# Thin fp32 products of a hybrid decoder block: one 128-row matmul instead of two 64-row matmuls

## Chip, cores and metric

One core of a Trainium2 chip runs the whole program; the seven others are idle. The metric is device time in microseconds of one execution. The engines are named as in the profile: PE is TensorE (PEld its weight loads), DVE is VectorE, ACT is ScalarE, POOL is GpSimd, SP is SyncE.

## The reference, cut

2048 tokens of width 1024 pass through one layer, all in fp32:

```
z  = rmsnorm(x) @ W_in                    # 1024 -> GLA heads | RWKV-7 heads
o  = concat(gla(z), rwkv7(z)) @ W_out;    h  = x + o
h += relu(rmsnorm(h) @ W1)^2 @ W2         # 1024 -> 4096 -> 1024
h += sigmoid(rmsnorm(h) @ W_g) * (p @ W_ple)
out = rmsnorm(h)
```

`gla` is gated linear attention with 4 heads (keys of 64, values of 128). `rwkv7` has 8 heads of 64 and the recurrence `S_t = S_{t-1} (diag(w_t) - kk_t^T (a_t kk_t)) + v_t^T k_t`. Both are computed in chunks with a carried state.

## The kernel before

The tokens form 4 blocks of 512; activations are held transposed, features on partitions and 512 tokens along the free dimension. Each large product is a `panel` (L287): 8 pieces of the contraction, each three matmuls in float32r (`mm3`, L278 to L280: high by high, high by low, low by high), 128x128 weights against 512 columns. So PE's stream is mostly L278, L279, L280 over and over.

A program of units sets the order. Per block these are the projection (`z_units`, tiles named z0 to z3), the output projection (o0 to o3), the feed-forward part (f0 to f3) and the gated embedding (p0 to p3). The chunked mixers are cut into small steps (`rwkv_units`, tiles r00 to r33; `gla_units`, g00 to g33; the digits are block and job, 16 jobs of 128 tokens each). A `tick` after each half panel lets the mixers' next steps in, so short groups of small matmuls stand between panels. The mixers of block 0 run beside the projections of blocks 1 to 3 (up to about 850 us); those of blocks 1, 2 and 3 beside the o, f and p parts of blocks 0, 1 and 2; the last block's o, f and p run alone.

The small fp32 products with 128 output rows went through a helper, `thin` (L282 to L284), which splits the 128 stationary columns in two: output rows 0 to 63 and 64 to 127, one matmul each. Four places call it:

- `Norm.sums` (L316): 4 products per call with one moving column (`ones1`). It gives the sums of squares of an RMSNorm; 16 calls, 4 per block.
- the post step of `rw_k` (L485): 4 products per call with 2 moving columns (`bo2`); 16 calls, all in the projections.
- `load` of `gla_units` (L627): 2 products with 2 moving columns, 16 calls; four transposes (L638) follow it.
- `chain` of `rwkv_units` (L955): 8 products, one per head, with 64 moving columns: the state and values in `P2` (tiles rpe, rpo) under weights in `W2` (rwe, rwo). 2 chains per job, 32 calls. ACT then copies the result (L957).

In the trace every fp32 matmul is two records on PE and two weight loads on PEld, one for each of its passes; float32r has one. Other small products that matter here use the array in other ways: L652 (128 stationary columns, 128 moving, fp32, full array), L735 (64 stationary columns), L638 and L763 (transposes by the identity).

Of the kernel before, what the change touches and what calls it, by code (L numbers as in the profile page):

```python
# [17 lines left out]
P = 128  # L18
# [43 lines left out]
def tile_hybrid_block(ctx: ExitStack, tc: tile.TileContext, a: dict, out: bass.AP):  # L62
    nc = tc.nc
    V, A, G, T = nc.vector, nc.scalar, nc.gpsimd, nc.tensor
# [7 lines left out]
    def st(shape, tag, bufs, dtype=F32):  # L72
        counter[0] += 1
        return sb.tile(shape, dtype, tag=tag, bufs=bufs, name=f"{stage[0]}.{tag}_{counter[0]}")
# [6 lines left out]
    def g2(n=TB):  # L81
        return st([P, 520], "g2", 10)[:, :n]
# [7 lines left out]
    def gx(n=512):  # L90
        return pt("gx", 4, n)

    def ct(shape, name, dtype=F32):
        return const.tile(shape, dtype, tag=name, name=name)
# [18 lines left out]
    ones1 = ct([P, 1], "ones1")  # L113
# [5 lines left out]
    bo2 = ct([P, 2], "bo2")  # L119
# [11 lines left out]
    for half in range(2):  # L131
        for q in range(4):
            m = mask[64 * half : 64 * half + 64, 64 * q : 64 * q + 64]
# [83 lines left out]
    def rsqrt(v, n, tag):  # L217
        half = st([P, n], tag + "i", 1, I32)
        V.tensor_scalar(half, v.bitcast(I32), 1, None, ALU.logical_shift_right)
        yi = st([P, n], tag + "y", 2, I32)  # L220
        V.tensor_scalar(yi, half, -1, RSQRT_MAGIC, ALU.mult, ALU.add)
        y = yi.bitcast(F32)
        t = st([P, n], tag + "t", 1)
        for _ in range(3):
            V.tensor_tensor(out=t, in0=y, in1=y, op=ALU.mult)
            V.scalar_tensor_tensor(t, t, -0.5, v, ALU.mult, ALU.mult)
            V.scalar_tensor_tensor(y, t, 1.5, y, ALU.add, ALU.mult)
        return y
# [50 lines left out]
        T.matmul(acc, wh, xs[1], start=False, stop=False)  # L279
        T.matmul(acc, wl, xs[0], start=False, stop=stop)  # L280

    def thin(acc, w, x):  # L282
        for m in (0, 64):
            T.matmul(acc[m : m + 64], w[:, m : m + 64], x, start=True, stop=True)  # L284

    def panel(w, xs, m=P):
        acc = pt("mm", 4)  # L287
        for k in range(KT):
            mm3(acc[:m], w, k, xs[k], k == 0, k == KT - 1, m)
            if k == KT // 2 - 1:  # L290
                tick()
        return acc

    class Norm:
# [18 lines left out]
        def sums(self):  # L313
            c = gx(4)
            for t in range(4):
                thin(c[:, t : t + 1], self.acc[:, t * P : t * P + P], ones1)  # L316
            v = st([P, 4], "nv", 2)
            V.tensor_scalar(v, c, 1.0 / D, EPS, ALU.mult, ALU.add)
            self.y = rsqrt(v, 4, "nr")
# [15 lines left out]
    def z_units(b):  # L335
# [37 lines left out]
        def project(m=P):  # L373
            return panel(take_w(), z["xs"], m)
# [99 lines left out]
        def rw_k(p):  # L474
            def f():
                k = shift(normed(project()), P, RW_K - RW_R + p)
                cols = slice(p * P, p * P + P)

                kq = g2()
                A.activation(kq, k, AF.Square, scale=vc("k_k", p))  # L480

                def post():
                    sp = gx(8)
                    for t in range(4):
                        thin(sp[:, 2 * t : 2 * t + 2], kq[:, t * P : t * P + P], bo2)  # L485
                    v = st([P, 8], "rnv", 1)
                    V.tensor_scalar(v, sp, 1e-24, None, ALU.max)
                    iv = rsqrt(v, 8, "rr")
                    ib = g2()
                    V.tensor_copy(ib.rearrange("p (t e) -> p t e", e=64), iv.unsqueeze(2).to_broadcast([P, 8, 64]))  # L490
                    pa = gx()
                    T.matmul(pa, a2s[:, cols], z["as"], start=True, stop=True)
                    an = g2()
                    A.activation(an, pa, AF.Tanh, bias=a0h[:, p : p + 1], scale=0.5)
                    kf = g2()
                    A.activation(kf, an, AF.Identity, bias=ka1[:, p : p + 1], scale=kah[:, p : p + 1])
                    A.activation(an, an, AF.Copy, bias=-0.5, scale=-0.5)
                    V.tensor_tensor(out=kf, in0=kf, in1=k, op=ALU.mult)
                    yield
                    ivb = gx()  # L500
                    for t in range(4):
                        T.transpose(ivb[:, t * P : t * P + P], ib[:, t * P : t * P + P], ident)
                    kkn = g2()
                    V.scalar_tensor_tensor(kkn, k, vc("k_k", p), ivb, ALU.mult, ALU.mult)
                    V.tensor_tensor(out=an, in0=an, in1=kkn, op=ALU.mult)
                    z["kkn"], z["an"], z["kf"] = kkn, an, kf

                return post

            return f  # L510
# [99 lines left out]
    def gla_units(b, j):  # L610
# [4 lines left out]
        def load():  # L615
            q, k, bb = (st([P, 2, P], n, 1) for n in ("gq", "gk", "gb"))
            ld(q, d_gq[b][:, :, js])
            ld(k, d_gk[b][:, :, js])
            ld(bb, d_gb[b][:, :, js])
            v = st([P, 4, P], "gv", 1)  # L620
            ld(v, d_gv[b][:, :, js])
            s_.update(q=q, k=k, b=bb)
            dp = gx(4)
            qk = st([P, 2, P], "gqk", 3)
            V.tensor_tensor(out=qk, in0=q, in1=k, op=ALU.mult)
            for i in range(2):
                thin(dp[:, 2 * i : 2 * i + 2], qk[:, i], bo2)  # L627
            ds = st([P, 4], "gds", 1)
            V.tensor_copy(ds, dp)
            S_ = st([P, 4, P], "gS", 1)  # L630
            V.tensor_tensor(
                out=S_, in0=ident.unsqueeze(1).to_broadcast([P, 4, P]),
                in1=ds.unsqueeze(2).to_broadcast([P, 4, P]), op=ALU.mult,
            )
            s_["S"] = S_
            bank = gx()
            for h in range(4):
                T.transpose(bank[:, h * P : h * P + P], v[:, h], ident)  # L638
            vt = st([P, 4, P], "gvt", 1)
            A.copy(vt.rearrange("p h e -> p (h e)"), bank)  # L640
            s_["vt"] = vt
# [142 lines left out]
    def rwkv_units(b, j):  # L784
# [158 lines left out]
        def chain(c):  # L943
            def f():
                yr, xr = halves[c], halves[1 - c]
                P2 = (s_["pe"], s_["po"])
                W2 = (s_["we"], s_["wo"])
                heads = [(h, *divmod(h, 2)) for h in range(8)]
                if c == 0:
                    A.copy(P2[0][lo, 0], rst[lo])  # L950
                    A.copy(P2[1][hi, 0], rst[hi])
                    s_["y"] = st([P, 512], "ry", 1)
                xy = pt("gx", 4)
                for h, p, e in heads:
                    thin(xy[:, h * 64 : h * 64 + 64], W2[e][:, p, c], P2[e][:, c, p])  # L955
                xs = st([P, 512], "rxs", 1)
                A.copy(xs, xy)  # L957
                yield
                ub = pt("gx", 4, 256)
                for h, p, e in heads:  # L960
                    T.matmul(ub[halves[e], p * 64 : p * 64 + 64], TT[xr, h], xs[xr, h * 64 : h * 64 + 64], start=True, stop=True)
                uv = ub.rearrange("z (p e) -> z p e", p=4)
                A.copy(P2[0][lo, c], uv[lo])
                V.tensor_copy(P2[1][hi, c], uv[hi])
                yield
                db = gx(256)
                for h, p, e in heads:
                    T.matmul(db[halves[e], p * 64 : p * 64 + 64], s_["bkt"][:, p, c, e], P2[e][:, c, p], start=True, stop=True)
                wt = st([P, 4, 64], "rwt", 1)
                V.tensor_tensor(out=wt, in0=rst, in1=db.rearrange("z (p e) -> z p e", p=4), op=ALU.add)  # L970
                pcb = pcs[b][:, :, 2 * j + c : 2 * j + c + 1].to_broadcast([P, 4, 64])
                if c == 0:
                    V.tensor_tensor(out=P2[0][lo, 1], in0=wt[lo], in1=pcb[lo], op=ALU.mult)
                    V.tensor_tensor(out=P2[1][hi, 1], in0=wt[hi], in1=pcb[hi], op=ALU.mult)
                V.tensor_tensor(out=rst, in0=wt, in1=pcb, op=ALU.mult)
                y2 = gx(256)
                for h, p, e in heads:
                    er = halves[e]
                    T.matmul(y2[er, p * 64 : p * 64 + 64], s_["gb"][er, p, c, 64 * c : 64 * c + 64], P2[e][er, c, p], start=True, stop=True)
                for e in range(2):  # L980
                    V.tensor_tensor(
                        out=hv(s_["y"][yr])[:, e], in0=hv(xs[yr])[:, e],
                        in1=y2[halves[e]].rearrange("z (p n) -> z p n", n=64), op=ALU.add)

            return f
# [338 lines left out]
```

## Time and profile before

| | |
|---|---|
| median of 3 runs | 2967.32 us (2962.82 to 2969.42) |
| the profiled execution | 2965.06 us, span 2963.4 us |
| PE busy | 2861.0 us (97%) |
| DVE, ACT busy | 2213.3 us (75%), 1189.7 us (40%) |
| granted TensorE clock, mean | 0.984 |
| fp32 records on the helper's line L284 | 1664 on PE, 1664 on PEld |

A matmul's record begins when it is dispatched and ends as the profile models it; records overlap. How long a group of matmuls holds PE is therefore read from the starts: from the start of the last panel matmul ahead of it to the start of the second panel matmul behind it, less the two panel steps that would have been there without it.

### The profile page before, as it was taken

To read this page: it belongs to the slowest core of one execution; us is meant where nothing else is said; L and a number is where in the kernel's file an instruction comes from. 1 tells how busy PE (TensorE), PEld (TensorE's weight loads), DVE (VectorE), ACT (ScalarE), POOL (GpSimd) and SP (SyncE) were. 2 spreads that over 40 slices of the span, in tenths; PEclk is the share of its full clock that TensorE was granted. 3 is DMA by queue.
4 is the path that set the end of the run, shared out by engine and by line. 5 is a ranking of instruction groups with operands and counts; after the bars stand their busy time and mean duration, and the time that the engine had idled before them with its cause. 6 is when DMAs were issued, how large, how long until landed. Compare 5 with 4: busy or idle time off the path is not lost.

```text
span 2963.4 us, 46550 instructions
## 1 busy us (share of the span) xinstructions
PE 2861.0 (97%) x16856; PEld 2264.1 (76%) x16856; DVE 2213.3 (75%) x5417; ACT 1189.7 (40%) x2230; POOL 114.1 (4%) x321
## 2 busy tenths in 40 slices
PE   7889999999999999999999999999999999999997
PEld 5667777777777877787777878777878787888886
DVE  6878786968797767788877868797867787544455
ACT  5435445444343333344433334443333344322233
POOL 4330000000000000000000000000000000000000
PEclk9999999999999999999999999999999999999999
DMA  7896877776754333334533333454333334322222
GB/s 277 291 310 207 251 231 224 244 231 211 231 182 121 106 117 114 115 111 154 147 113 110 111 116 107 127 176 118 109 116 114 103 108 164 100 94 99 93 94 78
DMA packets 332552, 453.63 MB, mean 153 GB/s; under 512 B 134096, under 2 KB 216064, under 8 KB 332320
## 3 DMA queue, kind: packets, MB, share of 16 engines
q1 hardware_dynamic: 324832, 423.38, 46.1%
q0 software_dynamic: 7488, 27.27, 2.3%
q8 instruction: 133, 2.18, 0.3%
q14 instruction: 99, 0.81, 0.1%
HBM read 357.21 MB, written 93.32 MB: 152 GB/s over the span
## 4 chain that ended last, share of the span: by engine, by line
PE 65%; DVE 7%; DMA 1%; issue 1%; SPq 1%; ACT 1%; DVEq 0%; ACTq 0%
PE f1.mm L278 4%; PE f3.mm L279 4%; PE f3.mm L278 4%; PE f3.mm L280 4%; PE f1.mm L280 4%; PE f1.mm L279 4%; PE f0.mm L278 3%; PE f2.mm L278 3%; PE f2.mm L280 3%; PE f2.mm L279 3%; PE f0.mm L280 3%; PE f0.mm L279 3%; PE p0.mm L278 1%; PE p1.mm L278 1%; PE p3.mm L278 1%
## 5 line engine op out<-in xcount | busy, mean ns | idle before, releaser
L251 ACT CAST f3.w<-f3.wr 128x512 fp32r<-128x512 f32 x128 | 79.6, 622 | 204.6 <-PE f3.mm L280 197.8
L251 ACT CAST f0.w<-f0.wr 128x512 fp32r<-128x512 f32 x128 | 79.1, 618 | 165.9 <-PE f0.mm L280 129.7
L251 ACT CAST f2.w<-f2.wr 128x512 fp32r<-128x512 f32 x128 | 79.0, 618 | 153.3 <-PE f2.mm L280 128.4
L251 ACT CAST f1.w<-f1.wr 128x512 fp32r<-128x512 f32 x128 | 79.0, 618 | 152.8 <-PE f1.mm L280 126.5
L254 DVE TENSOR_TENSOR f3.w<-f3.wr,f3.w 128x512 fp32r<-128x512 f32 x128 | 88.6, 692 | 63.1 <-ACT f3.w L251 59.8
L254 DVE TENSOR_TENSOR f0.w<-f0.wr,f0.w 128x512 fp32r<-128x512 f32 x128 | 88.0, 687 | 27.6 <-ACT f0.w L251 27.1
L254 DVE TENSOR_TENSOR f1.w<-f1.wr,f1.w 128x512 fp32r<-128x512 f32 x128 | 87.9, 686 | 24.5 <-ACT f1.w L251 23.9
L254 DVE TENSOR_TENSOR f2.w<-f2.wr,f2.w 128x512 fp32r<-128x512 f32 x128 | 87.9, 687 | 24.1 <-ACT f2.w L251 23.4
L278 PE MATMUL f1.mm<-f1.x,f1.w 128*128 128x512 f32 x256 | 103.7, 405 | 0.0
L278 PE MATMUL f2.mm<-f2.x,f2.w 128*128 128x512 f32 x256 | 103.6, 405 | 0.0
L278 PE MATMUL f0.mm<-f0.x,f0.w 128*128 128x512 f32 x256 | 103.5, 404 | 0.0
L280 PE MATMUL f1.mm<-f1.x,f1.w 128*128 128x512 f32 x256 | 101.4, 396 | 0.0
L280 PE MATMUL f0.mm<-f0.x,f0.w 128*128 128x512 f32 x256 | 101.3, 396 | 0.0
L279 PE MATMUL f1.mm<-f1.x,f1.w 128*128 128x512 f32 x256 | 101.1, 395 | 0.0
L280 PE MATMUL f2.mm<-f2.x,f2.w 128*128 128x512 f32 x256 | 101.1, 395 | 0.0
L279 PE MATMUL f0.mm<-f0.x,f0.w 128*128 128x512 f32 x256 | 100.9, 394 | 0.0
L280 PE MATMUL f3.mm<-f3.x,f3.w 128*128 128x512 f32 x256 | 100.8, 394 | 0.0
L278 PE MATMUL f3.mm<-f3.x,f3.w 128*128 128x512 f32 x256 | 100.7, 394 | 0.0
L279 PE MATMUL f2.mm<-f2.x,f2.w 128*128 128x512 f32 x256 | 100.7, 393 | 0.0
L278 PE MATMUL f0.mm<-o0.x,f0.w 128*128 128x512 f32 x248 | 100.7, 406 | 0.0
L279 PE MATMUL f3.mm<-f3.x,f3.w 128*128 128x512 f32 x256 | 100.6, 393 | 0.0
L278 PE MATMUL f2.mm<-o2.x,f2.w 128*128 128x512 f32 x248 | 100.2, 404 | 0.0
(2799 smaller groups left out, 8844.5 us busy)
## 6 DMA issues: line engine op xcount, KB each, us to landing
f0.wr<-w SPq DMA_DIRECT2D x63, 512.0 KB, 3.4
f1.wr<-w SPq DMA_DIRECT2D x63, 512.0 KB, 3.4
f2.wr<-w SPq DMA_DIRECT2D x63, 512.0 KB, 3.4
f3.wr<-w SPq DMA_DIRECT2D x63, 512.0 KB, 3.3
wc<-z0.w POOLq DMA_DIRECT2D x52, 512.0 KB, 5.5
z1.w<-wc SPq DMA_DIRECT2D x52, 512.0 KB, 5.3
z2.w<-wc SPq DMA_DIRECT2D x52, 512.0 KB, 4.8
z3.w<-wc SPq DMA_DIRECT2D x50, 512.0 KB, 4.4
```

Source lines behind the costliest of these rows:

```text
L251: A.copy(t[:, :512], r)
L254: eng.tensor_tensor(out=t[:, 512:], in0=r, in1=t[:, :512], op=ALU.subtract)
L278: T.matmul(acc, wh, xs[0], start=start, stop=False)
L279: T.matmul(acc, wh, xs[1], start=False, stop=False)
L280: T.matmul(acc, wl, xs[0], start=False, stop=stop)
```

## The change

The helper goes, and each of its four callers issues one matmul with all 128 stationary columns and all 128 output rows. Operands, moving columns, output places and the number of products stay; 832 half matmuls become 416 whole ones.

```diff
-    def thin(acc, w, x):
-        for m in (0, 64):
-            T.matmul(acc[m : m + 64], w[:, m : m + 64], x, start=True, stop=True)
...
-                thin(c[:, t : t + 1], self.acc[:, t * P : t * P + P], ones1)
+                T.matmul(c[:, t : t + 1], self.acc[:, t * P : t * P + P], ones1, start=True, stop=True)
...
-                        thin(sp[:, 2 * t : 2 * t + 2], kq[:, t * P : t * P + P], bo2)
+                        T.matmul(sp[:, 2 * t : 2 * t + 2], kq[:, t * P : t * P + P], bo2, start=True, stop=True)
...
-                thin(dp[:, 2 * i : 2 * i + 2], qk[:, i], bo2)
+                T.matmul(dp[:, 2 * i : 2 * i + 2], qk[:, i], bo2, start=True, stop=True)
...
-                    thin(xy[:, h * 64 : h * 64 + 64], W2[e][:, p, c], P2[e][:, c, p])
+                    T.matmul(xy[:, h * 64 : h * 64 + 64], W2[e][:, p, c], P2[e][:, c, p], start=True, stop=True)
```

Four lines fewer shift every later line number by 4: L955 is L951 after the change.

A scheduler decides where the small groups stand. It leaves the groups in their places beside the panels but for shifts by a panel matmul or two, nearly all in the projections. On PE, in the feed-forward part of block 0, a chain's eight products stand between two panel matmuls. Before (sizes are output rows x moving columns; f0.mm is a panel's accumulator, r10.gx the chain's result):

```order
L280 MATMUL f0.mm_9824<-o0.x_9422,f0.w_9735 128x512
L284 MATMUL r10.gx_9879<-r10.rpe_8884,r10.rwe_8867 64x64 x2
L284 MATMUL r10.gx_9879<-r10.rpo_8885,r10.rwo_8868 64x64 x2
L284 MATMUL r10.gx_9879<-r10.rpe_8884,r10.rwe_8867 64x64 x2
L284 MATMUL r10.gx_9879<-r10.rpo_8885,r10.rwo_8868 64x64 x2
...
L278 MATMUL f0.mm_9906<-o0.x_8928,f0.w_9816 128x512
```

And the same place with the change:

```order
L280 MATMUL f0.mm_9666<-o0.x_9268,f0.w_9577 128x512
L951 MATMUL r10.gx_9721<-r10.rpe_8732,r10.rwe_8715 128x64
L951 MATMUL r10.gx_9721<-r10.rpo_8733,r10.rwo_8716 128x64
L951 MATMUL r10.gx_9721<-r10.rpe_8732,r10.rwe_8715 128x64
L951 MATMUL r10.gx_9721<-r10.rpo_8733,r10.rwo_8716 128x64
...
L278 MATMUL f0.mm_9740<-o0.x_8774,f0.w_9658 128x512
```

The group keeps its place; each pair of 64-row matmuls has become one of 128 rows.

In four jobs the chain's group stands right behind another group with 64 stationary columns (L735, L731 after the change), here on PE in the gated embedding of block 0. Before:

```order
L731 MATMUL g13.gx_13809<-gst,g13.gqk_13663 128x128
L735 MATMUL g13.gx_13818<-g13.gvt_12936,g13.gk_13659 64x128 x4
L284 MATMUL r13.gx_13881<-r13.rpe_12910,r13.rwe_12893 64x64 x2
L284 MATMUL r13.gx_13881<-r13.rpo_12911,r13.rwo_12894 64x64 x2
```

With the change:

```order
L727 MATMUL g13.gx_13597<-gst,g13.gqk_13451 128x128
L731 MATMUL g13.gx_13606<-g13.gvt_12724,g13.gk_13447 64x128 x4
L951 MATMUL r13.gx_13669<-r13.rpe_12700,r13.rwe_12683 128x64
L951 MATMUL r13.gx_13669<-r13.rpo_12701,r13.rwo_12684 128x64
```

The neighbours are the same; only the chain's matmuls now have 128 rows behind a group of 64.

## Rows read from the trace of the kernel before

**Rows 1.** The profile's page: its first line, the busy times of three engines, and the granted clock in 40 slices (9 is 90% or more).

```profile
span 2963.4 us, 46550 instructions
PE 2861.0 (97%) x16856; PEld 2264.1 (76%) x16856; DVE 2213.3 (75%) x5417; ACT 1189.7 (40%) x2230; POOL 114.1 (4%) x321
PEclk9999999999999999999999999999999999999999
```

**Rows 2.** Busy time of each engine in two stretches, up to 850 us and behind it: us, then busy us and records of PE, PEld, DVE, ACT and POOL, granted clock, DMA share, GB/s.

```profile
0.00:850.00 850.00, 777.10 (x4544) 599.61 (x4545) 661.09 (x1693) 400.25 (x748) 103.99 (x254) 0.96 0.76 245
850.00:2963.40 2113.40, 2083.92 (x12314) 1664.46 (x12312) 1552.18 (x3725) 789.44 (x1483) 10.07 (x67) 0.99 0.38 116
```

**Rows 3.** Long waits of PE up to 850 us, one for each kind of releaser: who waited for whom, us in total, times, longest.

```profile
PE z1.gx L325 <- DVE z1.nry L227: 7.4, 1, 7.4
PE z0.mm L278 <- ACT z0.h L271: 7.1, 1, 7.1
PE z2.mm L278 <- DMA z2.w<-wc: 5.7, 2, 5.1
```

**Rows 4.** The longest waits of PE from 850 us on, and the three that follow the final norms of blocks 0 to 2; columns as in rows 3.

```profile
PE p2.gx L284 <- DVE p2.nacc L306: 3.5, 1, 3.5
PE p3.gx L284 <- DVE p3.nacc L306: 3.1, 1, 3.1
...
PE o1.mm L278 <- ACT o1.x L268: 1.0, 1, 1.0
PE o2.mm L278 <- ACT o2.x L268: 0.9, 1, 0.9
PE o3.mm L278 <- ACT o3.x L268: 0.9, 1, 0.9
```

**Rows 5.** The helper's line alone, L284, in the same two stretches: busy us and records of PE and of PEld, granted clock, DMA.

```profile
0.00:850.00 850.00, 25.66 (x616) 22.50 (x616) 0.96 0.76 245
850.00:2963.40 2113.40, 39.89 (x1048) 35.04 (x1048) 0.99 0.38 116
```

**Rows 6.** PE in order of time at a chain's group (start us, us, line, tiles, stationary rows*columns, moving size, count of merged records).

```profile
926.49 0.39 PE L280 MATMUL f0.mm<-o0.x,f0.w 128*128 128x512 f32 x1
926.81 0.34 PE L284 MATMUL r10.gx<-r10.rpe,r10.rwe 128*64 128x64 f32 x4
926.97 0.29 PE L284 MATMUL r10.gx<-r10.rpo,r10.rwo 128*64 128x64 f32 x4
...
927.67 0.29 PE L284 MATMUL r10.gx<-r10.rpo,r10.rwo 128*64 128x64 f32 x4
927.89 0.50 PE L278 MATMUL f0.mm<-o0.x,f0.w 128*128 128x512 f32 x1
928.23 0.39 PE L279 MATMUL f0.mm<-o0.x,f0.w 128*128 128x512 f32 x1
928.46 0.39 PE L280 MATMUL f0.mm<-o0.x,f0.w 128*128 128x512 f32 x1
```

**Rows 7.** The same view at a norm's sums, between two panels.

```profile
1870.99 0.40 PE L280 MATMUL p1.mm<-f1.x,f1.w 128*128 128x512 f32 x1
1871.31 0.63 PE L284 MATMUL p1.gx<-ones,f1.nacc 128*64 128x1 f32 x16
1871.88 0.50 PE L278 MATMUL p1.mm<-f1.x,p1.w 128*128 128x512 f32 x1
1872.21 0.39 PE L279 MATMUL p1.mm<-f1.x,p1.w 128*128 128x512 f32 x1
```

**Rows 8.** The same view at two fp32 products of the full array (four passes), L652.

```profile
1153.13 0.40 PE L280 MATMUL f0.mm<-o0.x,f0.w 128*128 128x512 f32 x1
1153.36 0.61 PE L652 MATMUL g12.gx<-qz,g12.gqk 128*128 128x128 f32 x4
1153.73 0.48 PE L278 MATMUL f0.mm<-f0.x,f0.w 128*128 128x512 f32 x1
1154.04 0.39 PE L279 MATMUL f0.mm<-f0.x,f0.w 128*128 128x512 f32 x1
```

**Rows 9.** Weight loads by line from 850 us on: duration in ns (shortest, median, longest), first and last start, stationary rows*columns. A chain's, a level's, and a transpose's.

```profile
L284 PEld LDWEIGHTS r10.gx<-r10.rpe,r10.rwe x32: 133/138/138, 926.8 to 942.2; 128*64 128x64 f32 x32
L652 PEld LDWEIGHTS g12.gx<-qz,g12.gqk x20: 187/192/192, 1125.8 to 1153.6; 128*128 128x128 f32 x20
L763 PEld LDWEIGHTS g10.gx<-ident,g10.gv x4: 138/140/142, 953.1 to 953.4; 128*128 128x128 f32 x4
```

**Rows 10.** PE in order of time where a chain's group stands behind L735.

```profile
1318.93 0.66 PE L735 MATMUL g13.gx<-g13.gvt,g13.gk 128*64 128x128 f32 x8
1319.42 0.28 PE L284 MATMUL r13.gx<-r13.rpe,r13.rwe 128*64 128x64 f32 x4
```

**Rows 11.** PE in order of time at a GLA job's load, with the transposes behind it.

```profile
1098.06 0.40 PE L280 MATMUL f0.mm<-f0.x,f0.w 128*128 128x512 f32 x1
1098.39 0.40 PE L284 MATMUL g12.gx<-bo,g12.gqk 128*64 128x2 f32 x8
1098.72 0.66 PE L638 MATMUL g12.gx<-ident,g12.gv 128*128 128x128 f32 x4
```

**Rows 12.** All engines in order of time at the last norm, near the end of the span.

```profile
2949.18 0.65 PE L284 MATMUL p3.gx<-ones,p3.nacc 128*64 128x1 f32 x16 [3.06 <-DVE p3.nacc L306]
2949.87 0.16 DVE L318 TENSOR_SCALAR p3.nv<-p3.gx 128x4 f32<-128x4 f32 x1 [0.83 <-PE p3.gx L284]
```

## The prediction, made before the result was known

> **What bounds the kernel now.** I read the page first: PE is busy 97% of the span and no other engine over 75% [rows 1]. A busy share of pipelined matmuls does not yet mean that PE is the bound, so I split the span where the projections end and looked at PE's waits on either side. From 850 us on PE is busy 2083.9 of 2113.4 us [rows 2], and its longest waits are of 1 to 3.5 us, at norms and at the seams between blocks [rows 4]. Up to 850 us it is busy 777 of 850 us [rows 2], and waits for DVE, ACT and DMA in turn [rows 3]. So in the last 2113 us a microsecond more or less of PE's time is nearly a microsecond of the run; in the first 850 us part of it only changes how long PE waits. The clock is close to full in both stretches (0.96, 0.99).
>
> The edit touches 1664 records on PE, 616 in the first stretch and 1048 in the second [rows 5]. Their busy time, 65 us, is no price: records overlap. I price a group from the starts, as the section on the profile says, with a panel step of 0.23 us (928.23 to 928.46 [rows 6]).
>
> **What a group costs today.**
>
> - A chain, 8 products: from 926.49 to 928.23 is 1.74 us; less two panel steps, 1.28 us [rows 6]. Inside it a product takes (927.67 - 926.97) / 6 = 0.117 us. That is two passes, each a pair of half matmuls; the four records of a product fit into 0.117 us only if the two halves of a pass run side by side. So a pair takes 0.058 us, 16 of them 0.93 us, and the remaining 0.35 us is what it costs to enter and leave the split array.
> - A norm's sums, 4 products: 1870.99 to 1872.21, less 0.46, is 0.76 us [rows 7]. The 16 calls in `rw_k` have the same 4 products, with 2 moving columns instead of 1; I price them alike.
> - A GLA load, 2 products: the panel ahead would be done at 1098.06 + 0.23 = 1098.29, and the transposes begin at 1098.72 [rows 11]: 0.43 us, called 0.45 with the transposes' first weight load.
>
> Rule beside the row: the Trainium skill, "TensorEngine Tiling (Array Packing)", section "Key Properties", says that tiles of the array can load weights and multiply in parallel, and that a change of tiling mode drains the engine. It speaks against this edit with its first half and for it with its second. By the drain alone a chain would fall by its 0.35 us; the rows above show both halves of the rule, and a pair at 0.058 us is the larger matter.
>
> **What it costs with the change.** Each pair of half matmuls becomes one pass of the full array: 832 passes where there were 832 pairs. Nothing in this kernel has 128 fp32 stationary columns under 64 or fewer moving columns, so the price of such a pass needs bounds.
>
> - From above: L652 has the same 128 fp32 stationary columns, and 128 moving. Four passes take 1154.04 - 1153.13 - 0.46 = 0.45 us [rows 8], 0.112 us a pass, with nothing for entering or leaving.
> - From below: 0.058 us, if the time of a pass went with its moving columns alone and a load of 128 columns hid as one of 64 does.
> - Which of the two: a load record of 64 columns takes 138 ns, one of 128 takes 192 ns [rows 9]. The 54 ns between them is close to the 58 ns of a pair, so 64 columns cost some 54 ns of loading and 128 some 108 ns. Every pass has its own load: there are as many loads as passes [rows 5]. If full-width loads come one after the other, as L652's 0.112 us a pass leaves room for just one, then the loads set the pace where the multiplying is short. A second sign: the first panel step after the chain is 0.34 us (927.89 to 928.23) instead of 0.23, 0.11 us more, the panel's own load of 128 columns with nothing to hide behind [rows 6]. I take 0.112 us.
>
> The cost of each call then: a chain 16 x 0.112 = 1.79 us instead of 1.28 (+0.51); sums and `rw_k` 8 x 0.112 = 0.89 instead of 0.76 (+0.13); a GLA load 4 x 0.112 = 0.45, no change. The 0.35 us of entering and leaving does go; doubling the pass costs 16 x 0.054 = 0.86 us in a chain. The price at which the whole edit breaks even comes from the same rows: today 32 chains x 1.28 + 32 x 0.76 + 16 x 0.45 = 72.5 us, less 1.4 for the joined chains below, over 832 passes is 0.085 us a pass.
>
> Four chains stand right behind L735, which has 64 stationary columns as well [rows 10]; they enter no new mode and share the leaving, so today they cost about 0.35 us less, an estimate from the chain's remainder. With the change the kernel leaves the split array at L735 whatever follows, so these four lose another 0.35 us each.
>
> **The sum.** From 850 us on there are 24 chains, 12 sums and 11 GLA loads: 24 x 32 + 12 x 16 + 11 x 8 = 1048 records, as counted [rows 5]. Four of the sums are the final norms of the blocks, eight stand inside the stream of panels. Chains +12.2 us, three joined ones +1.1, eight sums +1.0. Of the final norms three are followed by a wait of PE of 0.9 to 1.0 us for ACT [rows 4], which covers their +0.13. The last one is a chain of its own: PE starts cold at 2949.18 and DVE reads at 2949.87 [rows 12]; 8 passes at 0.112 instead of 0.058 make +0.4. Together +14.7 us.
>
> Up to 850 us: 8 chains, one of them joined (+4.1 and +0.35), 16 calls in `rw_k` and 4 sums (20 x 0.13 = +2.6), 5 GLA loads: +7.0 us of PE's time. PE has 73 us without work there [rows 2], but part of its waiting is for work that itself waits for these products (the longest, 7.4 us, is for the DVE steps behind a norm's sums [rows 3]), and such a wait moves with them. I count half, +3.5; all and nothing are its ends.
>
> Sum: +18.2 us. On the profiled execution 2965.1 + 18.2 = 2983.3 us; the median of the runs stands 2.3 us higher, so the predicted median is 2985 us, 0.6% slower. The other engines get the same instructions; the few moved by a panel step in the projections are left at zero, covered there by PE's 73 us of slack.
>
> **The rivals.**
>
> 1. *The count of matmuls sets the time, not the load: faster.* A full pass takes 0.058 us like a pair, and the 0.35 us per group goes. 832 x (0.085 - 0.058) = 22 us of gain: 2945 us. It decides below 0.085 us a pass. For it: L763's loads have 128 columns and take 140 ns, no longer than those of 64 [rows 9], so a 128-column load can be short. Against it: those are transposes; L652's loads, which are ordinary fp32 ones, take 192 ns. 9%. By the Trainium skill, "TensorEngine Tiling (Array Packing)", section "Instruction Overhead", every matmul carries about 60 cycles, and one moving column takes as long as 60; that rule would make half as many matmuls half the time, which is this rival. The trace bears it out only in that one moving column costs (0.76 - 0.35) / 8 = 0.051 us a pair today, close to the 0.058 of 64 [rows 6, 7].
> 2. *It washes out: within 0.2%.* A pass of about 0.08 to 0.09 us, say because the second pass of a product loads faster than the first, or most of the first stretch's cost hidden as well: 2967 us, give or take 6. For it: half of the first stretch is a guess. Against it: no row shows a pass of that price. 7%.
> 3. *Load and multiplication of a full pass don't overlap: much slower.* 0.108 + 0.058 = 0.166 us a pass; 512 passes of chains at 0.054 more than forecast add 28 us: 3013 us. Against it: L652 fits load and multiplication of 128 columns into 0.112 us [rows 8]. 3%.
>
> That the edit does something else than it says I leave out of the cases: the listing shows 128 output rows in one matmul at each of the four places.
>
> **How the numbers follow.** The forecast holds 81%. Its own range: 0.109 us a pass and the first stretch wholly hidden give +13 us, nothing hidden +22; on runs that lie between 2963 and 2969, 2976 to 2991. The 80% range goes a little beyond on both sides, for rival 2 and for the moved groups: 2973 to 2993 us. About 0.2%, 6 us, is what a measurement of this kernel tells from no change. Slower by more: forecast and rival 3, 84%. Within: 7%. Faster by more: 9%.
>
> **What would show it.** PE and PEld should have 832 records fewer (16024 left). Weight loads on the four lines should last about 190 ns, not 138. Chains should cost about 1.79 us from panel to panel, sums 0.89 us, GLA loads what they do now; from 850 us on the span should be some 14 to 15 us longer, before that 0 to 7. Loads of 140 ns and a chain of 0.93 us would prove rival 1, a chain near 2.6 us rival 3; chains at 1.79 us with an unchanged span would mean that PE is not the bound where I said it is.

## The result, and the profile after

The changed kernel takes 2989.78 us (median of four runs, 2985.16 to 2991.64), the kernel before beside it 2967.93 us (four runs, 2962.82 to 2969.42): a ratio of 1.0074, with an interval of 1.0057 to 1.0092, or 21.9 us more (17 to 27). Forecast was 2985.0 us. The profiled execution took 2991.36 us.

The page of the kernel after, first line and three engines; it answers to [rows 1]:

```profile
span 2989.7 us, 44889 instructions
PE 2897.1 (97%) x16024; PEld 2318.1 (78%) x16024; DVE 2207.5 (74%) x5417; ACT 1190.3 (40%) x2230; POOL 115.6 (4%) x321
```

832 records of PE are gone (16856 to 16024), and PE is busy 36 us longer. To see where, I cut both profiles at the same point of the program: the first panel matmul of the output projection of block 0 (o0), 836.9 us in the kernel before and 850.3 us in the one after. Columns as in [rows 2]. The kernel before, cut there:

```profile
0.00:836.90 836.90, 764.01 (x4486) 589.66 (x4486) 648.56 (x1672) 393.11 (x735) 103.99 (x254) 0.96 0.76 245
836.90:2963.40 2126.50, 2097.00 (x12370) 1674.41 (x12370) 1564.70 (x3745) 796.58 (x1495) 10.07 (x67) 0.99 0.38 117
```

The kernel after:

```profile
0.00:850.30 850.30, 783.88 (x4180) 614.54 (x4180) 643.93 (x1672) 393.36 (x735) 105.58 (x254) 0.95 0.75 242
850.30:2989.70 2139.40, 2113.22 (x11844) 1703.52 (x11844) 1563.61 (x3745) 796.95 (x1495) 10.06 (x67) 0.99 0.38 116
```

The second stretch is 12.9 us longer at the same clock, the first 13.4 us longer at a lower one, with PE busy 19.9 us more there and idle 6.5 us less (72.9 to 66.4).

The weight loads of the kernel after, columns as in [rows 9]: a chain's, a norm's sums', a GLA load's.

```profile
L951 PEld LDWEIGHTS r10.gx<-r10.rpe,r10.rwe x16: 187/192/192, 939.9 to 956.6; 128*128 128x128 f32 x16
L312 PEld LDWEIGHTS f0.gx<-ones,o0.nacc x8: 188/192/192, 905.5 to 906.4; 128*128 128x128 f32 x8
L623 PEld LDWEIGHTS g12.gx<-bo,g12.gqk x4: 188/190/192, 1113.3 to 1113.8; 128*128 128x128 f32 x4
```

The same groups on PE in order of time, columns as in [rows 6]: the chain of [rows 6], the GLA load of [rows 11] and the sums of [rows 7].

```profile
939.89 0.40 PE L280 MATMUL f0.mm<-o0.x,f0.w 128*128 128x512 f32 x1
940.12 0.33 PE L951 MATMUL r10.gx<-r10.rpe,r10.rwe 128*128 128x64 f32 x2
940.29 0.39 PE L951 MATMUL r10.gx<-r10.rpo,r10.rwo 128*128 128x64 f32 x2
...
941.63 0.39 PE L951 MATMUL r10.gx<-r10.rpo,r10.rwo 128*128 128x64 f32 x2
941.82 0.48 PE L278 MATMUL f0.mm<-o0.x,f0.w 128*128 128x512 f32 x1
942.14 0.39 PE L279 MATMUL f0.mm<-o0.x,f0.w 128*128 128x512 f32 x1
...
1113.32 0.39 PE L280 MATMUL f0.mm<-f0.x,f0.w 128*128 128x512 f32 x1
1113.55 0.50 PE L623 MATMUL g12.gx<-bo,g12.gqk 128*128 128x2 f32 x4
1113.91 0.63 PE L634 MATMUL g12.gx<-ident,g12.gv 128*128 128x128 f32 x4
1114.30 0.48 PE L278 MATMUL f0.mm<-f0.x,f0.w 128*128 128x512 f32 x1
1114.62 0.39 PE L279 MATMUL f0.mm<-f0.x,f0.w 128*128 128x512 f32 x1
...
1891.65 0.39 PE L280 MATMUL p1.mm<-f1.x,f1.w 128*128 128x512 f32 x1
1891.88 0.95 PE L312 MATMUL p1.gx<-ones,f1.nacc 128*128 128x1 f32 x8
1892.69 0.48 PE L278 MATMUL p1.mm<-f1.x,p1.w 128*128 128x512 f32 x1
1893.01 0.40 PE L279 MATMUL p1.mm<-f1.x,p1.w 128*128 128x512 f32 x1
```

Read as in the prediction, start to start less two panel steps: the chain takes 942.14 - 939.89 - 0.46 = 1.79 us (1.28 before), and (941.63 - 940.29) / 6 = 0.223 us a product, 0.112 us a pass. The sums take 0.90 us (0.76 before). The GLA load with its four transposes takes 1114.62 - 1113.32 - 0.46 = 0.84 us. Before, the same sequence ran from 1098.06 [rows 11] to the second panel matmul behind it,

```profile
1099.45 0.39 PE L279 MATMUL f0.mm<-f0.x,f0.w 128*128 128x512 f32 x1
```

0.93 us here, 0.925 in the median of nine.

### The profile page after: what moved, and what is told of

The parts are those of the page before. It is cut to its first block, busy times and chain, and to the rows that moved or that the text cites. A ratio compares the mean times of both kernels' runs of the same rounds, so it can differ in the third digit from the quotient of the medians.

```text
span 2989.7 us, 44889 instructions
## 1 busy us (share of the span) xinstructions
PE 2897.1 (97%) x16024; PEld 2318.1 (78%) x16024; DVE 2207.5 (74%) x5417; ACT 1190.3 (40%) x2230; POOL 115.6 (4%) x321
## 4 chain that ended last, share of the span: by engine, by line
PE 76%; DVE 9%; DMA 2%; ACT 2%; issue 1%; SPq 1%; DVEq 0%; ACTq 0%
PE f0.mm L278 4%; PE f3.mm L279 4%; PE f3.mm L278 4%; PE f3.mm L280 4%; PE f1.mm L278 4%; PE f0.mm L280 4%; PE f0.mm L279 4%; PE f1.mm L280 4%; PE f1.mm L279 4%; PE f2.mm L278 3%; PE f2.mm L280 3%; PE f2.mm L279 3%; PE z3.mm L278 1%; PE z3.mm L280 1%; PE z3.mm L279 1%
```

## Experiments

In all of them it was asked whether the load of 128 columns sets the pace of a narrow pass (my theory), or the count of matmuls, the moving columns, or the switch of the array; and then where the first stretch's time comes from. Costs of groups are medians over the groups between panels.

### Both kernels once more

Two unchanged copies, one execution each.

> The kernel before, profiled a second time, to see how far its first stretch (start to the first panel of the output projection, 836.9 us in the first profile) and its half-clock time there (64.6 us) move from execution to execution. If the 6 us by which the first stretch grew beyond the forecast are chance, this one should differ from 836.9 by several us; if they are the change's, by 1 to 2 us.

> The changed kernel, profiled a second time. First profile: first panel of the output projection at 850.3 us, the rest 2139.4 us, half-clock time in the first stretch 88.6 us. Chance: the first stretch comes out several us shorter or longer, with the half-clock time. The change's own doing: again 849 to 851 us and some 85 to 92 us at half clock. The rest: 2139 us by both.

They took 2966.88 and 2991.83 us. Cut at o0: 833.9 and 2131.2 us for the kernel before, 846.6 and 2143.5 us for the one after. Both stretches are longer again, by 12.7 and 12.3 us, so the first one's 13 us are not an accident of one profile.

### Only the chain, only the rest

```diff
-                    thin(xy[:, h * 64 : h * 64 + 64], W2[e][:, p, c], P2[e][:, c, p])
+                    T.matmul(xy[:, h * 64 : h * 64 + 64], W2[e][:, p, c], P2[e][:, c, p], start=True, stop=True)
```

is chain_full. small_full makes the same replacement at the sums, in `rw_k` and at the GLA load, and leaves the chain in halves.

> Only the chain's products with 128 output rows; sums, rw_k and GLA load in halves as before. Theory (a full-width load of 0.11 us sets the pace of a pass): chains 1.79 us instead of 1.28, 32 x 0.51 + 4 x 0.35 = +17.7 us, less what is hidden in the first stretch, so +14 to +18 us. Rival (the small products with 1 and 2 columns carry the loss): less than +8 us.

> The counterpart: sums, rw_k and GLA load with 128 output rows, chains in halves as before. Theory: sums and rw_k 32 x 0.13 = +4.2, GLA loads 16 x -0.085 = -1.4, so +2.8 us of PE time, of which the first stretch hides some: 0 to +3 us, within what can be measured. Rival (these products, whose results DVE waits for in the projections, stretch the first 850 us): +6 us or more, and a first stretch longer by that.

chain_full: 2982.70 us, ratio 1.0050 (1.0036 to 1.0064), 15 us. small_full: 2973.56 us, ratio 1.0012 (0.9997 to 1.0028), not told from no change; its runs spread from 2957 to 2979 us. The two parts make 0.62% together, the whole edit 0.74% (0.57 to 0.92). The chain carries the loss: 1.79 us in chain_full, 1.28 in small_full. In small_full the sums take 0.90 us and GLA load plus transposes 0.84, as in the kernel after.

### Halves that don't alternate

The chain keeps 64 output rows a matmul, but issues its eight upper halves and then its eight lower ones, so that neighbours no longer use different halves of the array.

```diff
-                for h, p, e in heads:
-                    thin(xy[:, h * 64 : h * 64 + 64], W2[e][:, p, c], P2[e][:, c, p])
+                for m in (0, 64):
+                    for h, p, e in heads:
+                        T.matmul(xy[m : m + 64, h * 64 : h * 64 + 64], W2[e][:, p, c, m : m + 64], P2[e][:, c, p], start=True, stop=True)
```

> The kernel before, with the chain's 64-row matmuls in another order: first the rows 0 to 63 of all eight heads, then the rows 64 to 127. Same matmuls, same count. Theory (two halves side by side, each load of 64 columns about 0.054 us): neighbours in the same half can't run side by side, a pass of one half takes 0.055 to 0.06 us by itself, 32 of them and 0.35 us make 2.1 to 2.2 us a chain instead of 1.28, +0.85 us x 32 = +22 to +28 us. Rival (a record costs 0.029 us whatever stands beside it): chains stay at 1.28 us and the time stays.

2992.0 us, ratio 1.0084 (1.0063 to 1.0105). The chain takes 2.03 us. PE of halves_in_turn at the chain of [rows 6]:

```profile
932.72 0.39 PE L280 MATMUL f0.mm<-o0.x,f0.w 128*128 128x512 f32 x1
...
933.78 0.33 PE L956 MATMUL r10.gx<-r10.rpe,r10.rwe 128*64 128x64 f32 x4
933.90 0.34 PE L956 MATMUL r10.gx<-r10.rpo,r10.rwo 128*64 128x64 f32 x4
934.07 0.28 PE L956 MATMUL r10.gx<-r10.rpe,r10.rwe 128*64 128x64 f32 x2
...
934.65 0.28 PE L956 MATMUL r10.gx<-r10.rpo,r10.rwo 128*64 128x64 f32 x2
...
935.21 0.39 PE L279 MATMUL f0.mm<-o0.x,f0.w 128*128 128x512 f32 x1
```

Within one half of the array a half product starts every (934.65 - 934.07) / 5 = 0.116 us, 0.058 us a half pass: as long as two half passes side by side take in the kernel before. Only where the last products of the first half meet the first of the second do they overlap: four of them share 0.29 us (933.78 to 934.07) instead of 0.47, which is why the chain stays under the 2.1 to 2.2 us expected. In all, the 32 passes of 64 columns that take 0.93 us alternating take 1.68 us here, plus the 0.35 for entering and leaving. So the split array by itself gains nothing here; it gains because two neighbours in different halves run side by side.

### Twice the moving columns

The kernel after, with up to 128 moving columns in a chain's products (twelve of its sixteen passes; the second half of each wide result is overwritten by the next product).

```diff
-                    T.matmul(xy[:, h * 64 : h * 64 + 64], W2[e][:, p, c], P2[e][:, c, p], start=True, stop=True)
+                    q = min(p + 2, 4)
+                    T.matmul(xy[:, h * 64 : h * 64 + 64 * (q - p)], W2[e][:, p, c], P2[e][:, c, p:q].rearrange("z q n -> z (q n)"), start=True, stop=True)
```

> The changed kernel, with 128 moving columns instead of 64 in six of a chain's eight products (the surplus half lands where the next head's product overwrites it). Theory (the load of 128 columns sets the pace): a chain stays at 1.79 us, the span within 2 us of 2990. Rival (the multiplication sets the pace): 12 of 16 passes go from 0.112 towards 0.2 us, +1 us a chain, +30 us.

2992.34 us in one execution against 2991.83 for the kernel after: the same. PE at the chain of [rows 6]:

```profile
937.37 0.40 PE L280 MATMUL f0.mm<-o0.x,f0.w 128*128 128x512 f32 x1
937.60 0.38 PE L952 MATMUL r10.gx<-r10.rpe,r10.rwe 128*128 128x128 f32 x2
...
939.30 0.48 PE L278 MATMUL f0.mm<-o0.x,f0.w 128*128 128x512 f32 x1
939.62 0.39 PE L279 MATMUL f0.mm<-o0.x,f0.w 128*128 128x512 f32 x1
```

939.62 - 937.37 - 0.46 = 1.79 us, not a hundredth more than with 64 columns. Up to 128 moving columns the multiplying is hidden behind the loading.

### Quarters

If the load is what a pass costs, then four quarters of 32 columns side by side should beat two halves. The sums and `rw_k` get four matmuls of 32 output rows a product; the chain keeps its halves, and the GLA load has 128 rows, which cost it less above.

```diff
     def thin(acc, w, x):
-        for m in (0, 64):
-            T.matmul(acc[m : m + 64], w[:, m : m + 64], x, start=True, stop=True)
+        n = 32 if x.shape[-1] < 8 else 64
+        for m in range(0, P, n):
+            T.matmul(acc[m : m + n], w[:, m : m + n], x, start=True, stop=True)
...
-                thin(dp[:, 2 * i : 2 * i + 2], qk[:, i], bo2)
+                T.matmul(dp[:, 2 * i : 2 * i + 2], qk[:, i], bo2, start=True, stop=True)
```

> A version drawn from the prices: chains in halves as before; GLA load in one matmul of 128 rows (0.40 us instead of 0.48); sums and rw_k in four matmuls of 32 rows. Theory (loads of columns in different parts of the array run side by side, a load takes as long as it has columns): a load of 32 columns takes 0.027 us, a pass of four 0.03 us, 8 passes and 0.35 us make 0.55 to 0.6 us instead of 0.76; with the GLA loads 32 x -0.18 and 16 x -0.085 = -7 us, 2960 us. Rival (the number of matmuls counts, 64 records a group instead of 32): 0.76 us or more, no gain or a loss of some us.

2959.14 us (12 runs, 2949.93 to 2966.33), ratio 0.9976 (0.9962 to 0.9989): 7 us faster than the kernel before, with 17304 matmul records instead of 16856. By the prices of the groups about 1.4 us of it is the GLA load's. PE and PEld at the sums of [rows 7]:

```profile
1864.09 0.40 PE L280 MATMUL p1.mm<-f1.x,f1.w 128*128 128x512 f32 x1
1864.42 0.43 PE L285 MATMUL p1.gx<-ones,f1.nacc 128*32 128x1 f32 x32
1864.78 0.50 PE L278 MATMUL p1.mm<-f1.x,p1.w 128*128 128x512 f32 x1
1865.12 0.39 PE L279 MATMUL p1.mm<-f1.x,p1.w 128*128 128x512 f32 x1
```

```profile
L285 PEld LDWEIGHTS p1.gx<-ones,f1.nacc x32: 106/113/113, 1864.4 to 1864.6; 128*32 128x32 f32 x32
```

The sums take 1865.12 - 1864.09 - 0.46 = 0.57 us: 0.90 in one piece, 0.76 in halves, 0.57 in quarters, the same products each time.

### Where the first stretch's time comes from

rwk_full has 128 rows in `rw_k` alone, sums_gla_full at the sums and the GLA load alone (the edits of small_full, one by one).

> Only the 16 groups of rw_k with 128 output rows, all in the projections; the rest in halves as before. By PE's time alone 16 x 0.13 = +2.1 us, part of it hidden: 0 to +2 us, first stretch 835 to 839 us. Theory (what the first stretch lost beyond the forecast comes with rw_k's passes of 2 moving columns at full width, by the clock or by the order around them): +5 us or more, first stretch 842 us or more with over 75 us of it at half clock.

> The counterpart: the norms' sums and the GLA load with 128 output rows, rw_k and chains in halves. By PE's time: 16 x 0.13 - 16 x 0.085 = +0.7 us, the final norm +0.3: no change to be measured. If the first stretch's loss comes with these (the sums stand behind long waits of PE): first stretch 842 us or more, +5 us.

2967.76 us, ratio 1.0008 (0.9998 to 1.0019), and 2968.23 us, ratio 1.0004 (0.9996 to 1.0013): neither is told from no change. Their first stretches were 839.0 us, with 71.7 us at half clock, and 839.6 us, with 75.1: neither reaches the 842 us that would have put the loss on it alone.

small_wide is small_full with 64 moving columns instead of 1 or 2 at its three places (only the columns needed are read; the results lie 64 columns apart, so DVE reads them with a stride), here for the sums, cut to the matmul:

```diff
-                thin(c[:, t : t + 1], self.acc[:, t * P : t * P + P], ones1)
+                T.matmul(c[:, 64 * t : 64 * t + 64], self.acc[:, t * P : t * P + P], ones[:, :64], start=True, stop=True)
```

> As small_full (sums, rw_k and GLA load with 128 rows, chains in halves), but with 64 moving columns in each of these products instead of 1 or 2; the surplus columns are not read. By the load theory the groups cost what they cost there (0.89 and 0.40 us). Theory of the first stretch (full-width passes with 1 or 2 moving columns leave the array so little to do that the clock falls to half behind them, without any idle time): with 64 columns the clock doesn't fall behind rw_k, half-clock time up to the first panel of the output projection goes from 88.7 us to 65 to 72 us, that panel starts at 838 to 842 us instead of 847. Rival (order of the instructions, or later results for DVE): first stretch 846 to 848 us as in small_full.

> small_full profiled a second time: first panel of the output projection at 847.0 us and 88.7 us at half clock ahead of it in the first profile. If this belongs to the kernel, again 845 us or more and 80 us or more; if it was chance, 836 to 843 us and about 65 to 72 us.

> small_wide profiled a second time: 840.5 us and 68.3 us at half clock in the first profile. If 64 moving columns keep the clock up, again 838 to 843 us and 65 to 72 us; if the first profile was chance, 845 us or more.

small_wide: 2973.99 us, ratio 1.0030 (1.0014 to 1.0046), no faster than small_full. Its groups cost the same (sums 0.90 us, GLA load and transposes 0.84): 1, 2 or 64 moving columns make no difference. The two copies took 2969.92 and 2974.25 us. small_full's first stretch was 847.0 us in one profile and 838.6 in the other, with 88.7 and 64.8 us at half clock, so a single profile of it can't be trusted to 8 us.

In the table the first stretch of each profile is taken apart by a sum. The first two columns are read (time up to o0 against 835.4, the mean of both profiles of before; time at half clock against 64.9 in both). The pass price is what the measured groups cost more (8 chains 0.51 and one joined 0.35; 20 sums and `rw_k` 0.13, in quarters -0.20; 5 GLA loads -0.085; halves in turn 0.75 a chain). At half clock a panel step takes 0.43 us instead of 0.24 (last section), so half of the added half-clock time is counted as lost, an estimate. The remainder is what the sum leaves over; no row shows it.

| profile | up to o0 | half clock | pass price | half of the half clock | remainder |
|---|---|---|---|---|---|
| after | +14.9 | +23.8 | +6.6 | +11.9 | -3.6 |
| after_again | +11.2 | +17.0 | +6.6 | +8.5 | -3.9 |
| moving_doubled | +12.2 | +20.4 | +6.6 | +10.2 | -4.6 |
| chain_full | +4.5 | +3.4 | +4.4 | +1.7 | -1.6 |
| small_full | +11.5 | +23.8 | +2.2 | +11.9 | -2.5 |
| small_full_again | +3.2 | -0.1 | +2.2 | 0 | +1.0 |
| rwk_full | +3.6 | +6.8 | +2.1 | +3.4 | -1.9 |
| sums_gla_full | +4.2 | +10.2 | +0.1 | +5.1 | -1.0 |
| halves_in_turn | +6.9 | +3.4 | +6.0 | +1.7 | -0.8 |
| quarters | -4.3 | 0 | -4.4 | 0 | +0.1 |
| small_wide | +5.1 | +3.4 | +2.2 | +1.7 | +1.2 |
| small_wide_again | +8.5 | 0 | +2.2 | 0 | +6.3 |

But for the last row the remainder is between -4.6 and +1.2 us. In the three profiles with everything at 128 rows it is -3.6 to -4.6, which would be pass price hidden in PE's waits. By this sum the first stretch's loss is mostly time at half clock. That is argued, not shown by an experiment: small_wide has 20 us less at half clock than the first profile of small_full and is no faster in its median, and of its second profile the sum leaves 6 us open.

What the clock costs can be read more widely, since the span and mean clock of every run are on record. Span times (1 - clock) is the time that the clock would cost if PE never waited. Its mean is 49.6 us in the 63 runs of the kernel before that were made beside the experiments, 55.3 in the four runs of the kernel after. The span less this time grew by 16.8 us from before to after (by 17.6 in chain_full, 24.0 in halves_in_turn, 0.7 in small_full, but 8.7 in small_wide, which nothing here explains). So of the 22 us some 6 go with the clock. This is an estimate: in the 12 runs of small_full a microsecond of that measure goes with 0.8 us of span.

Part of the half-clock time can be placed. Between 640 and 770 us, around the `rw_k` groups of the fourth projection, the six profiles in which `rw_k` has 128 rows and 2 moving columns have 13.7 to 17.1 us at half clock. The eight others have 0 to 10.2, seven of them 3.4 at most, among them both of small_wide, with 128 rows and 64 moving columns. rwk_full there (clock 0.95), then small_wide (0.99), columns as in [rows 2]:

```profile
640.00:770.00 130.00, 125.12 (x675) 97.63 (x674) 100.25 (x308) 62.03 (x118) 2.78 (x14) 0.95 0.69 220
640.00:770.00 130.00, 125.43 (x703) 97.20 (x702) 101.73 (x311) 64.43 (x122) 2.54 (x14) 0.99 0.73 229
```

Up to 640 us no such pattern stands: there profiles of one kernel differ by as much (small_full 68.3 and 44.4 us at half clock). Why the kernel after has more in all its profiles is not settled beyond this, nor is small_wide_again, whose 843.9 us lie in neither of the ranges expected.

## Why the prediction was right, and where it was off

- **A pass of 128 columns costs its load, 0.112 us.** Right: 1.79 us a chain in 24 groups (1.78 to 1.80), loads of 192 ns, and no change with the moving columns from 64 to 128. Rival 1 falls by the same rows, rival 3 too: its chain would have taken near 2.6 us. Rival 2, within 0.2%, falls by the ratio, 1.0057 at the least. Stationary columns are output rows as well, and no run parts the two; the load is named because its record grows by the same 54 ns as the pass. By the Trainium skill, "TensorEngine Tiling (Array Packing)", section "Instruction Overhead", one moving column takes as long as 60; the runs agree (1, 2 and 64 columns cost alike), and here 128 cost no more. That section of the Trainium skill also advises against taking a tiling factor from a dimension that is already small. No run tests that: the pieces (0.90, 0.76, 0.57 us for one, two, four) split the 128 stationary columns, not the few moving ones.
- **Two halves run side by side at 0.058 us a pair, 0.35 us to enter and leave.** Right: in turn the halves take 0.058 us each, as long as a pair. The joined chains lost 0.85 us each (sequences of 5.73, 5.73 and 5.68 us, before 4.88, 4.88 and 4.82), 0.51 + 0.35 as forecast. The last norm, in order of time after (columns as in [rows 12]): 2976.18 - 2975.11 = 1.07 us, before 0.69, +0.38 where +0.4 was forecast.

```profile
2975.11 1.02 PE L312 MATMUL p3.gx<-ones,p3.nacc 128*128 128x1 f32 x8 [3.05 <-DVE p3.nacc L302]
2976.18 0.16 DVE L314 TENSOR_SCALAR p3.nv<-p3.gx 128x4 f32<-128x4 f32 x1 [1.21 <-PE p3.gx L312]
```

- **Sums +0.13, GLA loads 0.** The sums: right, 0.90 us between panels and +0.13 for `rw_k` where it stands alone. GLA loads: they gain 0.085 us each. The prediction looked only up to the transposes' start, not at the whole sequence, and so put the term at nothing. From 850 us on that is 11 x 0.085 = 0.9 us less.
- **From 850 us on +14.7.** With the GLA term 13.7 by the group costs; measured 2139.4, 2143.5 and 2143.0 (moving_doubled) against 2126.5 and 2131.2, +13.1 between the means, at nearly the same time at half clock (33.9 and 34.6 us in the mean). Right, as was the reading that PE bounds this stretch [rows 2, 4].
- **Up to 850 us +3.5, ends 0 and 7.** This is the term that was mis-sized: +11 to +15 us. The pass price in it was right (+6.6 by the measured groups against +7.0). That PE's waits hid half of it fits the remainders of the table (-3.6 to -4.6), but only a sum says so. What was left out is the clock: the prediction took 0.96 [rows 2] as given. With the edit 17 to 24 us more pass at half clock in the three profiles, by the table 8.5 to 12 us of lost work, more than the whole pass price; over all runs the clock's share is nearer 6 us. The bound "nothing hidden" was no bound.
- **The sum.** +18.2 forecast; 13.1 + 12.8 = 25.9 us between the means of the profiles (three and two), 21.9 between the medians, which lies 3.7 above the sum. Less the clock's time the spans grew by 16.8 us, so the sum of passes was right in size and the clock is what it lacked. The terms of the two stretches missed in opposite directions (-1.6 us behind 850 us, some +9 up to it), so that the total came nearer than the larger miss is in part luck. (2983.3 + 2.3 is 2985.6; the prediction wrote 2985, which decides nothing.)

## What to carry to other kernels

For an fp32 product with few moving columns, count the columns of stationary data that must be loaded one after the other, not the matmuls: splitting the output rows over halves or quarters of the array pays as soon as the group has enough passes to cover 0.35 us of entering and leaving (here two products don't, four do), and only if neighbours alternate between the pieces. Fewer instructions on the busiest engine are no gain by themselves. Where an engine with waits also changes its clock, its slack is no bound on what added work costs there.

## What was not expected of the hardware

The granted clock fell to half not only behind waits. In both profiles of small_full it fell, with no wait of PE just ahead, behind eight full passes of `rw_k` with two moving columns that follow L820's group of 64 stationary rows. PE in the first profile of small_full in order of time, then two windows (columns as in [rows 2]):

```profile
701.07 1.16 PE L820 MATMUL r03.gx<-r03.rwo,r03.rbk 64*128 64x128 f32 x8
702.15 1.05 PE L485 MATMUL z3.gx<-bo,z3.g 128*128 128x2 f32 x8
703.07 0.48 PE L492 MATMUL z3.gx<-z3.x,c.x 96*128 96x512 f32 x1
703.38 0.40 PE L280 MATMUL z3.mm<-z3.x,z3.w 128*128 128x512 f32 x1
703.62 0.46 PE L278 MATMUL z3.mm<-z3.x,z3.w 128*128 128x512 f32 x1
703.88 0.63 PE L279 MATMUL z3.mm<-z3.x,z3.w 128*128 128x512 f32 x1
704.31 0.63 PE L280 MATMUL z3.mm<-z3.x,z3.w 128*128 128x512 f32 x1
```

```profile
694.00:704.00 10.00, 10.00 (x59) 7.85 (x58) 9.42 (x23) 4.06 (x9) 0.25 (x1) 0.99 0.85 275
704.00:714.00 10.00, 10.00 (x30) 7.41 (x29) 6.17 (x23) 1.34 (x4) 0.00 (x0) 0.50 0.25 67
```

PE is busy all 20 us; the panel step goes from 0.24 to 0.43 us, and the granted clock from full to 0.50 (1.2 GHz). The same place in small_wide, with 64 moving columns in L485, keeps the full clock (1.00 from 702 to 712 us).

Up to o0 the 14 profiles have five falls with PE busy throughout just ahead: two in each profile of small_full and one in rwk_full (at 317.7 us). All five come soon after an `rw_k` group of eight full passes with two moving columns; every other fall follows a wait of PE. As small_wide was no faster in its median, what such a fall costs a run is not shown.

Time at half clock also differs between executions of one kernel: 64.8 and 88.7 us in small_full's first stretch, whose runs lie 22 us apart (2957.08 us at a mean clock of 0.986, 2979.07 at 0.979).
